# A bidirectional scan on one core: keys and queries of a half head in one tile, and a copy moved to ScalarE

## The chip, the core and the metric

The kernel runs on one core of a Trainium2 chip. A core has five engines, each with a queue of its own that is worked off in order: TensorE (PE in the profile; PEld is its loading of weights), VectorE (DVE), ScalarE (ACT), GpSimd (POOL) and SyncE (SP), which here issues most of the DMAs. Engines meet at semaphores only. The metric is the device time of one execution in microseconds; the time before is a median of three runs. Tiles lie in SBUF, 128 partitions wide; TensorE writes to PSUM, which is handed out here in banks of 128 x 512 float32.

## What is computed

One layer of a hybrid encoder over 1024 positions of width 1024: a norm, one large projection, a convolution module, a bidirectional gated scan over 8 heads of 128, a gated merge, and a feed-forward part. The change lies in the scan. For each head and direction, cut from the reference:

```python
def step(state, inp):                       # one chunk of 64 positions
    qb, kb, vb, lfb = inp
    a = jnp.cumsum(lfb, axis=2)             # lf = log f, f the forget gate
    diff = a[:, :, :, None, :] - a[:, :, None, :, :]
    decay = jnp.where(tril, jnp.exp(jnp.minimum(diff, 0.0)), 0.0)
    scores = jnp.einsum("bhtk,bhsk,bhtsk->bhts", qb, kb, decay)
    o = (jnp.einsum("bhts,bhsv->bhtv", scores, vb)
         + jnp.einsum("bhtk,bhkv->bhtv", qb * jnp.exp(a), state))
    ...
o_fwd = _chunk_gated_scan(qh, heads(k_f), vh, heads(lf_f))
o_bwd = flip(_chunk_gated_scan(flip(qh), flip(heads(k_b)), flip(vh), flip(heads(lf_b))))
return o_fwd + o_bwd
```

So a score of query t and key s carries the product of the forget gates between them, for each of 128 channels; the forward direction takes s up to t, the backward one the rest, and the two sums are added.

## The kernel before

The scan (lines 1053 to 1418) works on half heads: 512 positions of one head, channels on the partitions, both directions at once. There are 16 of them (i = 0 to 15). Four generators work on each.

*scan_inputs* (L1053) loads q and the two gate tiles z (page "zi", three buffers), and ScalarE makes from them the key gates kk (L1064) and the forget gates f (L1065, L1067), which VectorE clamps (L1074). It is called two half heads ahead.

*scan_base* (L1077) works out decays within blocks of 8 positions. All of it is on VectorE. DE holds, for both directions, running products from the middle of each block outwards (E, rows 0 to 3 and on) and the same for D; one buffer for all half heads. The first instruction of a base copies two rows of f into DE (L1092); the second (written as the first tt, L1093) multiplies two rows of f; the third (L1095, in the profile DE<-f,DE) goes on from there, the fourth (L1096) finishes the block products, and the reciprocal (L1098) turns them round. Then come fm, the table tb of block decays, the remaining rows of DE, the scaled queries Qh and keys Kh, and last the queries qF and the keys kG, each a tile of two rows of 512: qF[:, 1] holds the queries of the forward and qF[:, 0] those of the backward direction, kG[:, d] the keys of direction d. qF has three buffers (the outputs of the head read it late), kG two. The helper tt writes every such product at L1042, so the profile names these groups by their tiles.

*scan_levels* (L1137) makes the scores. Within blocks of 8, TensorE multiplies Qh and Kh (inside, L1174). Then for h = 8, 16, 32, 64 it multiplies the keys of each block of h with the queries of its neighbour. At h = 8 and 16 (level, L1157) ScalarE first gathers the keys of a level into a tile A (L1160), and TensorE multiplies A with views of qF (L1162), into a bank "sc" at 8 and "ob" at 16. At 32 and 64 (blocks, L1182) it reads kG and qF directly (L1188). After each level the keys and queries are multiplied by the decay over the neighbouring block, half the blocks of each direction, 512 elements each (L1213 for the keys, L1214 for the queries), and the table is halved (L1222). Masked copies (L1226 to L1230) gather the scores of the lower levels from the banks into D.

*scan_states* (L1238) transposes the updated keys (TensorE L1245, ScalarE's copy kT L1247), multiplies them with the values (L1254, banks "ob" and "sc"), and carries the state: the forward states Sf on VectorE (L1260, L1262), the backward ones Sb copied by ScalarE (L1272, L1274) and carried by VectorE at the start of the outputs (L1347).

*scan_outputs* (L1277) multiplies scores and states (L1295, bank "ob", which has one buffer), takes the norm on ScalarE with GpSimd's power (L1300, L509, L510, L1314), transposes (L1321) and gates the result on VectorE (L1323).

What sets the order: TensorE's order is the program's (manual_schedule). After each step of levels and states, between() puts in 1.3 pieces of the stream "dense" on average (one piece is six 128 x 512 matmuls of the projection's last columns, L147 to L149), two steps of the next half head's base, and one step of the previous head's outputs. The other engines' orders are made when the program is built: a scheduler may move an instruction ahead of others on its engine where its operands allow. The weights of the dense stream are loaded by SP (L134, two buffers), split into a high and a low part by ScalarE and VectorE (L123), and its results are copied out by ScalarE (L720, L722).

The loop around it:

```python
def between(fill):
    dense.fill(fill)
    if ahead is not None:
        ahead.step(BASE_STEPS)
    pending.fill(1)
```

Of the kernel before, what the change touches and what calls it, by code (L numbers as in the profile page):

```python
# [10 lines left out]
F32 = mybir.dt.float32  # L11
# [7 lines left out]
P = 128  # L19
# [11 lines left out]
H = 512  # L31
# [15 lines left out]
def tile_hybrid_encoder(  # L47
# [45 lines left out]
    def nm(s):  # L93
        uid[0] += 1
        return f"{s}_{uid[0]}"
# [6 lines left out]
    def page(pool, tag, bufs, dt=F32):  # L102
        return pool.tile([P, H], dt, tag=tag, name=nm(tag), bufs=bufs)
# [949 lines left out]
    def scan_inputs(i):  # L1053


        h, half = divmod(i, 2)
        q = page(hp, "q", 2)
        f = hp.tile([P, 2, H], F32, tag="f", name=nm("f"), bufs=2)
        kk = hp.tile([P, 2, H], F32, tag="k", name=nm("k"), bufs=2)
        nc.sync.dma_start(q, d_q[h][half])  # L1060
        for d in range(2):
            z = page(hp, "zi", 3)
            nc.sync.dma_start(z, d_z[d][h][half])
# [3 lines left out]
            A.activation(  # L1067
                fo,
                z.rearrange("p (b e) -> p b e", e=8),
                AF.Identity,  # L1070
                scale=oml_of(d, h),
                bias=lb_of(d, h),
            )
        V.tensor_scalar(f, f, MIN_FORGET, 1.0, op0=ALU.max, op1=ALU.min)  # L1074
        return q, f, kk, kscale[:, h : h + NH + 1 : NH]

    def scan_base(ins):  # L1077


        q, f, kk, ks = ins  # L1080

        def two(t, *r):
            if len(r) == 1:
                return view(t, r[0], [[8, N2]])
            return view(t, r[0], [[r[1] - r[0], 2], [8, N2]])

        fv = lambda *r: two(f, *r)
        ed = lambda *r: two(DE, *r)
        D = D0


        V.tensor_copy(ed(2, D + 4), fv(3, 4))  # L1092
# [5 lines left out]
        V.reciprocal(ed(D, 7), ed(0, D + 7))  # L1098
# [36 lines left out]
        yield qF, kG, [(Qh[:, 1 - d, :], Kh[:, d, :]) for d in range(2)], tb  # L1135

    def scan_levels(base, S_t, Tt):  # L1137


        qF, kG, qk, tb = base  # L1140
# [16 lines left out]
        def level(b, h):  # L1157

            A_t = page(hp, "A", 2)
            A.copy(A_t.rearrange("p (b x e) -> p b x e", x=2, e=h), pairs(kG, h))  # L1160
            for at, g, o in each():
                T.matmul(  # L1162
                    b[g, o].rearrange("p (b x e) -> p b x e", x=2, e=h),
                    A_t[:, at : at + 32],
                    view(qF, at, [[2 * h, 16 // h], [H + h, 2], [1, h]]),
                    start=True,
                    stop=True,
                )
# [13 lines left out]
        def blocks(b, h):  # L1182

            for c in range(0, H, P):
                for s0 in range(0, P, h):
                    t0 = s0 ^ h
                    d = s0 // h % 2
                    T.matmul(  # L1188
                        b[s0 : s0 + h, c + t0 : c + t0 + h],
                        kG[:, d, c + s0 : c + s0 + h],  # L1190
                        qF[:, 1 - d, c + t0 : c + t0 + h],
                        start=True,
                        stop=True,
                    )
# [7 lines left out]
        for h in (8, 16, 32, 64):  # L1202
# [5 lines left out]
            else:  # L1208
# [1 line left out]
                    b = bank("sc")  # L1210
                    T.matmul(b, none[:, :P], none, start=True, stop=True)
                blocks(b, h)
            tt(pairs(kG, h), pairs(kG, h), view(tb, 1, [[2, n], [nb - 1, 2], [0, h]]))  # L1213
            tt(pairs(qF, h), pairs(qF, h), view(tb, nb + 1, [[2, n], [nb - 1, 2], [0, h]]))  # L1214
            if h < 64:
                tn = hp.tile([P, 3, NB], F32, tag="tb", name=nm("tb"), bufs=3)
                k = 3
# [17 lines left out]
                    A.copy(S_t[g : g + 32, :, g : g + 32], D_t[g : g + 32])  # L1235
            yield

    def scan_states(i, kG, v, Tt, Sf, Sb):  # L1238

        half = i % 2  # L1240
        kTs = []
        for d in range(2):
            b = bank("tr")
            for c in range(4):
                T.transpose(b[:, c * P : (c + 1) * P], kG[:, d, c * P : (c + 1) * P], ident)  # L1245
            kT = page(hp, "kT", 2)
            A.copy(kT, b)  # L1247
            kTs.append(kT)
            yield
# [27 lines left out]
    def scan_outputs(h, kept, Sf, Sb):  # L1277
# [3 lines left out]
        ss = cp.tile([P, 2, 4], F32, name=nm("oss"), tag="oss", bufs=2)  # L1281
        rs = cp.tile([P, 2, 4], F32, name=nm("ors"), tag="ors", bufs=2)
        for half in range(2):
            S_t, v, qF = kept[half]
            o = bank("ob")
            for c in range(4):
                sl = slice(c * P, (c + 1) * P)
                g = half * 4 + c
                terms = [(S_t[:, c, :], v[:, c, :])]
                if g > 0:  # L1290
                    terms.append((qF[:, 1, sl], Sf[half][:, c, :]))
                if g < 7:
                    terms.append((qF[:, 0, sl], Sb[half][:, c, :]))
                for n, (l, r) in enumerate(terms):
                    T.matmul(o[:, sl], l, r, start=(n == 0), stop=(n == len(terms) - 1))  # L1295
            on = tmp()
# [72 lines left out]
    for h in range(NH):  # L1369
# [4 lines left out]
        for half in range(2):  # L1374
# [13 lines left out]
            for n, _ in enumerate(scan_levels(base, S_t, Tt[:, half])):  # L1388
# [7 lines left out]
            qF, kG = base[0], base[1]  # L1396
            for _ in scan_states(i, kG, v, Tt, Sf, Sb):
                between(FILL)
            kept.append((S_t, v, qF))
            cur = ahead  # L1400
        pending = Stream(outputs(h, kept, Tt, Sf, Sb))

# [397 lines left out]
```

## Time and profile before

| | |
|---|---|
| time before, median of 3 runs (lowest to highest) | 1792.36 us (1791.06 to 1793.42) |
| span of the profiled execution | 1788.8 us |
| instructions | 27583 |
| granted TensorE clock, mean | 0.996 |
| the scan in the span | some 505 to 905 us |
| projections before it, merge and feed-forward after it | the rest |

The profiled execution's own time is not listed beside its span; the runs are 3.6 us above the span. On the page, a group is given by line, engine and operation, output tile <- input tiles, and partitions x elements of each; behind it busy time, mean duration in ns, and the engine's idle time just before with what ended it. In the timeline the columns are start and duration in us, engine, line, operation and tiles; a bracket names idle time before. Instructions of VectorE and ScalarE overlap a little in their records, so the time that one takes in a queue is read from start to start.

### The profile page before, as it was taken

Reading aid. Unit: us, or ns where it says so; the run is one execution under the profiler, and the core shown is the slowest. Engines: PE = TensorE matmul, PEld = TensorE weight load, DVE = VectorE, ACT = ScalarE, POOL = GpSimd, SP = SyncE. Lnnn points to the kernel's source line nnn. Section 1 sums busy time; section 2 is a strip of 40 time slices with the busy share of each in tenths; the row PEclk is TensorE's granted clock in tenths of the full one; section 3 lists DMA queues with packets and bytes.
Section 4 is the critical chain, followed back from the end, with each engine's and each line's share of the span. In section 5 each row is a group of like instructions: output and inputs, shape, how many; then the busy total and the mean of one; then the engine's idle time right before and its main releaser. Section 6 shows DMA issues by size and latency. Waiting matters only on the chain.

```text
span 1788.8 us, 27583 instructions
## 1 busy us (share of the span) xinstructions
PE 1733.0 (97%) x10632; PEld 1416.7 (79%) x10638; DVE 1250.4 (70%) x1884; ACT 775.0 (43%) x1490; POOL 153.8 (9%) x168
## 2 busy tenths in 40 slices
PE   8989999999999999999999999999999999999997
PEld 6878877888777777777778888878888888888885
DVE  5599999746569999999645557667667667544455
ACT  7344333334555566655442245344344344422123
POOL 2201111000000000000000002011111111000000
PEclk9999999999999999999999999999999999999999
DMA  8657887743663433333257665567667665534233
GB/s 285 216 151 187 185 185 185 199 150 126 199 214 101 125 119 119 119 119 101 90 180 219 200 201 177 153 142 159 151 144 158 142 151 133 161 103 126 79 91 135
DMA packets 317705, 276.41 MB, mean 155 GB/s; under 512 B 14462, under 2 KB 242566, under 8 KB 317574
## 3 DMA queue, kind: packets, MB, share of 16 engines
q1 hardware_dynamic: 276406, 242.15, 43.1%
q0 software_dynamic: 41168, 32.51, 12.6%
q8 instruction: 83, 1.36, 0.3%
q14 instruction: 48, 0.39, 0.1%
HBM read 185.73 MB, written 72.61 MB: 144 GB/s over the span
## 4 chain that ended last, share of the span: by engine, by line
PE 65%; DVE 19%; DMA 5%; issue 4%; ACT 4%; POOL 1%; SPq 0%; POOLq 0%; DVEq 0%; ACTq 0%
PE mm L147 16%; PE mm L148 16%; PE mm L149 16%; PE sc L147 3%; PE sc L149 3%; PE sc L148 3%; DVE acc L955 2%; DVE kG L1042 2%; DVE DE L1042 2%; DVE qF L1042 2%; DVE wp L123 2%; PE tr L147 1%; PE tr L149 1%; PE tr L148 1%; DVE DE L1098 1%
## 5 line engine op out<-in xcount | busy, mean ns | idle before, releaser
L147 PE MATMUL mm<-hx,wp 128*128 128x512 f32 x1128 | 454.8, 403 | 9.8 <-DVE ev L717 4.3
L149 PE MATMUL mm<-hx,wp 128*128 128x512 f32 x1128 | 441.7, 392 | 1.9 <-DVE wp L123 1.9
L148 PE MATMUL mm<-hx,wp 128*128 128x512 f32 x1128 | 441.4, 391 | 0.0
L123 ACT CAST wp<-wr 128x1024 fp32r<-128x1024 f32 (+2 forms) x179 | 167.0, 934 | 359.6 <-PE mm L148 271.5
L147 PEld LDWEIGHTS mm<-hx,wp 128*128 128x128 f32 x1128 | 212.5, 188 | 55.7 <-DVE ev L717 6.7
L123 DVE TENSOR_TENSOR wp<-wr,wp 128x1024 fp32r<-128x1024 f32 (+2 forms) x177 | 191.4, 1082 | 90.4 <-ACT wp L123 90.1
L149 PEld LDWEIGHTS mm<-hx,wp 128*128 128x128 f32 x1128 | 212.6, 188 | 49.3 <-DVE wp L123 3.2
L148 PEld LDWEIGHTS mm<-hx,wp 128*128 128x128 f32 x1128 | 212.9, 189 | 40.4 <-issue 0.2
L955 DVE SCALAR_TENSOR_TENSOR acc<-gl,v_b,acc 128x1024 f32<-128x1024 f32 x120 | 149.0, 1277 | 0.5
L1651 DVE TENSOR_TENSOR xr<-mm,xr 128x512 f32<-128x512 f32 x48 | 33.2, 691 | 73.1 <-PE mm L149 73.1
L367 ACT COPY su<-mm 128x512 f32<-128x512 f32 x78 | 45.2, 579 | 62.5 <-PE mm L149 61.5
L123 ACT CAST wq<-sw 128x1024 fp32r<-128x1024 f32 x39 | 41.0, 1051 | 64.4 <-issue 28.6
L1500 DVE SCALAR_TENSOR_TENSOR tm<-gp,v_a,tm 128x512 f32<-128x512 f32 x88 | 65.9, 749 | 2.0
L147 PE MATMUL mm<-hy,wp 128*128 128x512 f32 x156 | 61.5, 394 | 1.4 <-ACT su L367 1.4
L148 PE MATMUL mm<-hy,wp 128*128 128x512 f32 x156 | 61.1, 392 | 0.0
L147 PE MATMUL sc<-hy,wq 128*128 128x512 f32 x156 | 61.1, 392 | 0.0
L149 PE MATMUL sc<-hy,wq 128*128 128x512 f32 x156 | 61.1, 391 | 0.0
L147 PE MATMUL tr<-hx,wp 128*128 128x512 f32 x156 | 60.8, 390 | 0.0
L149 PE MATMUL tr<-hx,wp 128*128 128x512 f32 x156 | 60.7, 389 | 0.0
L148 PE MATMUL tr<-hx,wp 128*128 128x512 f32 x156 | 60.7, 389 | 0.0
L148 PE MATMUL sc<-hy,wq 128*128 128x512 f32 x156 | 60.7, 389 | 0.0
L149 PE MATMUL mm<-hy,wp 128*128 128x512 f32 x156 | 60.6, 389 | 0.0
(368 smaller groups left out, 3467.6 us busy)
## 6 DMA issues: line engine op xcount, KB each, us to landing
wr<-in_w_in_dram SPq DMA_DIRECT2D x56, 512.0 KB, 4.7
wr<-in_ffn_w_up_dram SPq DMA_DIRECT2D x24, 512.0 KB, 4.9
sw<-in_ffn_w_up_dram SPq DMA_DIRECT2D x44, 256.0 KB, 3.0
d_g<-ft SPq DMA_DIRECT2D x44, 256.0 KB, 2.7
sw<-in_ffn_w_up_dram POOLq DMA_DIRECT2D x20, 512.0 KB, 8.3
sw<-in_w_in_dram SPq DMA_DIRECT2D x34, 256.0 KB, 3.2
d_z<-ev SPq DMA_DIRECT2D x32, 256.0 KB, 3.1
zi<-d_z SPq DMA_DIRECT2D x32, 256.0 KB, 3.2
```

The source lines that it names most:

```text
L123: parts = A.copy(hi, src), eng.tensor_tensor(lo, src, hi.bitcast(F32), op=ALU.subtract)
L147: T.matmul(acc, whi[:, k, :], ahi, start=first, stop=False, skip_group_check=again)
L148: T.matmul(acc, whi[:, k, :], alo, start=False, stop=False, skip_group_check=again)
L149: T.matmul(acc, wlo[:, k, :], ahi, start=False, stop=last, skip_group_check=again)
L367: A.copy(t, acc)
L955: V.scalar_tensor_tensor(acc, g[:, k : k + S], tap(k), acc, op0=ALU.mult, op1=ALU.add)
L1042: V.tensor_tensor(o, a, b, op=op)
L1098: V.reciprocal(ed(D, 7), ed(0, D + 7))
L1500: V.scalar_tensor_tensor(c, g[:, o + k : o + k + H], vec("fdw", k * NF + j), c, op0=ALU.mult, op1=ALU.add,)
L1651: V.tensor_tensor(xr[i][half], acc, xr[i][half], op=ALU.add)
```

## The change

Keys and queries of a half head lie in one tile KQ of four rows, keys and queries by turns: row 0 the keys of the forward direction, row 1 the queries of the backward one, row 2 the keys of the backward, row 3 the queries of the forward direction. With that, the blocks that a level's update touches in the keys and in the queries form one regular view: pairs(h, n) runs over n steps of 2h, across two neighbouring rows, in rows 0 and 1 and, shifted by h, in rows 2 and 3. One instruction of 1024 elements takes the place of two of 512 after each level. KQ has three buffers (24 KB of each partition, where qF and kG took 20), and zi two in place of three. The copy at the start of a base goes from VectorE to ScalarE. What is computed stays the same.

```diff
@@ scan_inputs
-            z = page(hp, "zi", 3)
+            z = page(hp, "zi", 2)
@@ scan_base
-        V.tensor_copy(ed(2, D + 4), fv(3, 4))
+        A.copy(ed(2, D + 4), fv(3, 4))
         tt(ed(1, D + 5), fv(2, 4), fv(3, 5))
         yield
         tt(ed(0, D + 6), fv(1, 6), ed(1, D + 5))
...
-        qF = hp.tile([P, 2, H], F32, tag="qF", name=nm("qF"), bufs=3)
-        kG = hp.tile([P, 2, H], F32, tag="kG", name=nm("kG"), bufs=2)
+        KQ = hp.tile([P, 4, H], F32, tag="KQ", name=nm("KQ"), bufs=3)
...
-        both = [[H, 2], [8, NB], [1, 8]]
-        tt(view(qF, 0, both), view(Qh, 0, both), view(fm, 0, [[NB, 2], [1, NB], [0, 8]]))
+        both, apart = [[H, 2], [8, NB], [1, 8]], [[2 * H, 2], [8, NB], [1, 8]]
+        tt(view(KQ, H, apart), view(Qh, 0, both), view(fm, 0, [[NB, 2], [1, NB], [0, 8]]))
         yield
-        tt(view(kG, 0, both), view(Kh, 0, both), view(DE, D + 7, [[H, 2], [8, NB], [0, 8]]))
+        tt(view(KQ, 0, apart), view(Kh, 0, both), view(DE, D + 7, [[H, 2], [8, NB], [0, 8]]))
@@ scan_levels
-        def pairs(t, h):
-            return view(t, 0, [[2 * h, H // (2 * h)], [H + h, 2], [1, h]])
+        def pairs(h, n):
+            return view(KQ, 0, [[2 * h, n], [2 * H + h, 2], [1, h]])
...
-            A.copy(A_t.rearrange("p (b x e) -> p b x e", x=2, e=h), pairs(kG, h))
+            A.copy(A_t.rearrange("p (b x e) -> p b x e", x=2, e=h), pairs(h, H // (2 * h)))
...
-                    view(qF, at, [[2 * h, 16 // h], [H + h, 2], [1, h]]),
+                    view(KQ, H + at, [[2 * h, 16 // h], [2 * H + h, 2], [1, h]]),
...
-            tt(pairs(kG, h), pairs(kG, h), view(tb, 1, [[2, n], [nb - 1, 2], [0, h]]))
-            tt(pairs(qF, h), pairs(qF, h), view(tb, nb + 1, [[2, n], [nb - 1, 2], [0, h]]))
+            tt(pairs(h, nb), pairs(h, nb), view(tb, 1, [[2, nb], [nb - 1, 2], [0, h]]))
```

In blocks, scan_states and scan_outputs the views follow: kG[:, d] is KQ[:, 2 * d], qF[:, 1 - d] is KQ[:, 3 - 2 * d].

More of the change, by code (lines that the diff above doesn't have):

```diff
@@ L1129, in scan_base @@
             yield
-        both = [[H, 2], [8, NB], [1, 8]]
-        tt(view(qF, 0, both), view(Qh, 0, both), view(fm, 0, [[NB, 2], [1, NB], [0, 8]]))
+        both, apart = [[H, 2], [8, NB], [1, 8]], [[2 * H, 2], [8, NB], [1, 8]]
+        tt(view(KQ, H, apart), view(Qh, 0, both), view(fm, 0, [[NB, 2], [1, NB], [0, 8]]))
         yield
-        tt(view(kG, 0, both), view(Kh, 0, both), view(DE, D + 7, [[H, 2], [8, NB], [0, 8]]))
+        tt(view(KQ, 0, apart), view(Kh, 0, both), view(DE, D + 7, [[H, 2], [8, NB], [0, 8]]))
         yield
-        yield qF, kG, [(Qh[:, 1 - d, :], Kh[:, d, :]) for d in range(2)], tb
+        yield KQ, [(Qh[:, 1 - d, :], Kh[:, d, :]) for d in range(2)], tb
     def scan_levels(base, S_t, Tt):
-        qF, kG, qk, tb = base
-        def pairs(t, h):
-            return view(t, 0, [[2 * h, H // (2 * h)], [H + h, 2], [1, h]])
+        KQ, qk, tb = base
+        def pairs(h, n):
+            return view(KQ, 0, [[2 * h, n], [2 * H + h, 2], [1, h]])
         def near(t):
@@ L1236, in scan_levels, with scan_states @@
             yield
-    def scan_states(i, kG, v, Tt, Sf, Sb):
+    def scan_states(i, KQ, v, Tt, Sf, Sb):
         half = i % 2
@@ L1244, in scan_states @@
             for c in range(4):
-                T.transpose(b[:, c * P : (c + 1) * P], kG[:, d, c * P : (c + 1) * P], ident)
+                T.transpose(b[:, c * P : (c + 1) * P], KQ[:, 2 * d, c * P : (c + 1) * P], ident)
             kT = page(hp, "kT", 2)
@@ L1283, in scan_outputs @@
         for half in range(2):
-            S_t, v, qF = kept[half]
+            S_t, v, KQ = kept[half]
             o = bank("ob")
@@ L1290, in scan_outputs @@
                 if g > 0:
-                    terms.append((qF[:, 1, sl], Sf[half][:, c, :]))
+                    terms.append((KQ[:, 3, sl], Sf[half][:, c, :]))
                 if g < 7:
-                    terms.append((qF[:, 0, sl], Sb[half][:, c, :]))
+                    terms.append((KQ[:, 1, sl], Sb[half][:, c, :]))
                 for n, (l, r) in enumerate(terms):
@@ L1395, in tile_hybrid_encoder @@
                 between(FILL)
-            qF, kG = base[0], base[1]
-            for _ in scan_states(i, kG, v, Tt, Sf, Sb):
+            KQ = base[0]
+            for _ in scan_states(i, KQ, v, Tt, Sf, Sb):
                 between(FILL)
-            kept.append((S_t, v, qF))
+            kept.append((S_t, v, KQ))
             cur = ahead
```

4 lines of the change are left out of this document (2 added, 2 removed).

## The prediction

> **What bounds the kernel now.** I read the page first (first lines, then the strip of VectorE over the span), then the scan by stretches of 120 us, then who waited there.
>
> ```profile
> span 1788.8 us, 27583 instructions
> PE 1733.0 (97%) x10632; PEld 1416.7 (79%) x10638; DVE 1250.4 (70%) x1884; ACT 775.0 (43%) x1490; POOL 153.8 (9%) x168
> ...
> DVE  5599999746569999999645557667667667544455
> ```
>
> The whole span belongs to TensorE (97%). Only in two places is VectorE full; the second, slices 12 to 19, is the scan. The same stretch by windows (columns: stretch, length, then busy microseconds and instructions of each engine, clock, DMA):
>
> ```profile
> 520.00:640.00 120.00, 113.04 (x1419) 92.02 (x1421) 112.40 (x223) 70.73 (x166) 3.98 (x4) 1.00 0.38 115
> 640.00:760.00 120.00, 113.59 (x1527) 93.05 (x1527) 111.56 (x227) 71.27 (x172) 4.18 (x4) 1.00 0.40 124
> 760.00:880.00 120.00, 114.88 (x1486) 94.30 (x1487) 104.35 (x219) 65.48 (x174) 5.57 (x6) 1.00 0.31 100
> ```
>
> Two engines are nearly full at once: TensorE for 341.5 of 360 us, VectorE for 328.3; ScalarE is at 58%. The change leaves TensorE's instructions and their order as they are, so the time can move only through TensorE's idle time, 18.5 us here. What ended it, over the same 360 us (engine and line, what it waited for, us in total, times, longest):
>
> ```profile
> PE ob L1162 <- DVE qF L1042: 6.0, 7, 1.5
> PE tr L1245 <- DVE kG L1042: 4.9, 7, 1.8
> PE sc L1188 <- DVE qF L1042: 3.2, 6, 1.2
> PE ob L1295 <- DVE D L1230: 1.1, 1, 1.1
> PE sc L1254 <- ACT kT L1247: 0.9, 2, 0.5
> PE ob L1162 <- ACT wp L123: 0.9, 1, 0.9
> ```
>
> Nearly all of it is VectorE being late, in three places of a half head: before the matmuls of level 16 (6.9), before the key transposes (4.9), before levels 32 and 64 (3.2). Each is a wait between two engines, so it depends on where VectorE's work stands in its queue as well as on how much there is.
>
> **The change part by part.**
>
> ```profile
> L1042 DVE TENSOR_TENSOR qF<-qF,tb 128x512 f32<-128x512 f32 x62 | 42.4, 684 | 0.4 <-PE sc L1162 0.4
> L1042 DVE TENSOR_TENSOR kG<-kG,tb 128x512 f32<-128x512 f32 x62 | 42.2, 682 | 0.6 <-ACT A L1160 0.4
> ...
> L1160 ACT COPY A<-kG 128x512 f32<-128x512 f32 x32 | 19.7, 616 | 20.9 <-DVE kG L1042 20.8
> L1042 DVE TENSOR_TENSOR qF<-Qh,fm 128x1024 f32<-128x1024 f32 x16 | 19.5, 1218 | 0.0
> ...
> L1092 DVE COPY DE<-f 128x256 f32<-128x256 f32 x15 | 6.3, 418 | 0.0
> ...
> L1225 ACT COPY D<-sc 128x128 f32<-128x128 f32 x16 | 4.2, 265 | 5.8 <-PE sc L1162 5.7
> ```
>
> (The groups of the scan, mean ns behind the busy time.) *Work off VectorE.* 64 pairs of 512-element updates become 64 of 1024. By durations that is 683+683-1218 = 148 ns each. But a row runs on into the next one; what the queue gets back is start to start, from the timeline of the fifth half head:
>
> ```profile
> 610.25 1.21 DVE L1042 TENSOR_TENSOR kG<-Kh,DE 128x1024 f32<-128x1024 f32 x1
> 611.38 0.41 DVE L1092 COPY DE<-f 128x256 f32<-128x256 f32 x1
> 611.71 0.71 DVE L1042 TENSOR_TENSOR DE<-f 128x256 f32<-128x256 f32 x1
> ...
> 612.45 0.69 DVE L1042 TENSOR_TENSOR DE<-f,DE 128x256 f32<-128x256 f32 x1
> 613.18 0.40 DVE L1042 TENSOR_TENSOR DE<-DE,f 128x128 f32<-128x128 f32 x1
> 613.61 1.76 DVE L1098 RECIPROCAL DE<-DE 128x256 f32<-128x256 f32 x1
> 615.28 0.25 DVE L1262 SCALAR_TENSOR_TENSOR Sf<-Sf,Tt,ob 128x128 f32<-128x128 f32 x1
> ...
> 616.05 0.34 DVE L1262 SCALAR_TENSOR_TENSOR Sf<-Sf,Tt,ob 128x128 f32<-128x128 f32 x1
> 616.30 1.22 DVE L123 TENSOR_TENSOR wp<-wr,wp 128x1024 fp32r<-128x1024 f32 x1
> 617.44 0.34 DVE L1262 SCALAR_TENSOR_TENSOR Sf<-Sf,Tt,ob 128x128 f32<-128x128 f32 x1
> 617.70 0.69 DVE L1042 TENSOR_TENSOR kG<-kG,tb 128x512 f32<-128x512 f32 x1
> 618.30 0.34 DVE L1347 SCALAR_TENSOR_TENSOR Sb<-Sb,Tt 128x128 f32<-128x128 f32 x1
> ...
> 618.90 0.69 DVE L1042 TENSOR_TENSOR qF<-qF,tb 128x512 f32<-128x512 f32 x1
> ```
>
> 1024 elements take 1.13 us (610.25 to 611.38), 512 take 0.60 (617.70 to 618.30): 0.07 us a pair, 4.5 us for 64. The copy gives 0.33 (611.38 to 611.71), 5.3 for 16. Together 9.8 us, 0.6 for a half head. On ScalarE the copy costs between the 265 ns of 128 elements and the 616 of 512, taken at 0.38, so 6 us on an engine at 58%; its own load is no bound.
>
> *What the order makes of it.* In the program before, the keys' update of level 8 or 16 waits only for ScalarE's copy A; after, it rewrites the queries too and must wait for TensorE's level. And level 16 now runs through VectorE (level 8's merged update), ScalarE (copy A of level 16) and then TensorE. The bigger shift is the copy's: the third instruction of a base (the 612.45 row) waits, in the built program, for ScalarE's copy, which stands there behind copy A of the half head just begun. So in 12 of 15 half heads the built order puts that instruction, the next and the reciprocal behind the forward state update, where they stood ahead of it. That update waits for TensorE's state matmuls:
>
> ```profile
> 613.06 1.05 PE L1254 MATMUL ob<-v,kT 128*128 128x128 f32 x8
> ...
> 616.91 0.45 PE L1162 MATMUL sc<-qF,A 128*32 128x32 f32 x30
> ...
> 618.56 0.40 PE L149 MATMUL mm<-hx,wp 128*128 128x512 f32 x1
> 619.74 0.46 PE L1162 MATMUL ob<-qF,A 128*32 128x32 f32 x32 [0.78 <-DVE qF L1042]
> ```
>
> Before, the states end at 614.11, VectorE comes 1.17 us late to them (615.28) because it is finishing the reciprocal, and ends the queries' update at 619.59; TensorE, free at 618.96, waits 0.78. After: without copy, third and fourth instruction and reciprocal VectorE is there before 613.1 and idles. From 614.15 it does, start to start: three state updates (0.77), the weight split (1.14), third (0.73) and fourth (0.43) instruction, two backward updates (0.52), reciprocal (1.67), the merged update (1.21): 6.5 us, to 620.6. Copy A takes 0.62 and the handovers some 0.2: TensorE starts at 621.4, a wait of 2.4 for 0.78, so 1.6 more. Done so for each half head from the two built orders, the mean shift is 1.4 us. Six of the twelve have no slack there (they wait today): 8.4. In two, four transposes of the outputs stand in the gap, whose 0.53 us come off the shift, 0.9 each: 1.8.
>
> ```profile
> 645.02 0.60 PE L1321 MATMUL tr<-ident,tm 128*128 128x128 f32 x4
> 645.55 0.46 PE L1162 MATMUL ob<-qF,A 128*32 128x32 f32 x32
> ```
>
> Four have dense matmuls enough to hide it. Two that wait today and keep their order give back what the copy and a pair free, 0.4 each. **Term 1: +9.4.** Low end -3 (VectorE remains late at the states, the reorder costs nothing and the shorter queue gives half a microsecond in six), high end +20 (twelve pay 1.7 in full).
>
> *The bank "ob".* The output matmuls of the previous head wait until the masked copy has read level 16 (the row of 1.1). That copy now stands behind a merged update that can only start when level 16 is done: some 0.5 us late in seven half heads, less the 1.1 of today. **Term 2: +2.4**, from -1.1 to +5.
>
> *Waits that go.* A TensorE that is held at level 16 gives VectorE the time to be ready later: some 1.2 us (0.6 of work, and its update of level 8 ends earlier by copy A's 0.62 before TensorE's start). Against it the transposes wait for 1.13 us of update where they waited for the keys' 0.60. Of 4.9+3.2 us I take 6.5 away. **Term 3: -6.5**, from -8.1 to 0.
>
> The Trainium skill, page "Perfetto Trace Analysis", section "Optimizing Scalar/DVE Operations", has a rule for either side: larger operations help an engine that is saturated, while one that is not but leaves bubbles on others had better be given smaller ones, so that parts are done sooner. By the second half the update should have stayed in two: with 16 transposes each 0.53 later Term 3 would be +8.5, and the time 1812.7, which I count to the much slower cases below.
>
> *At nothing:* two buffers of zi for three, and KQ in three buffers.
>
> ```profile
> SPq L1063 <- ACT f L1067: 60.1, 25, 5.7
> ...
> ACT wp L123 <- PE mm L148: 11.1, 6, 3.8
> ```
>
> Between 480 and 900 us SP's queue already waits 60 us for a free zi, and the weight loads stand behind it; but ScalarE's split of weights waits for TensorE to free a page, not for a load. In the built order the weight load now comes ahead of most zi loads. Were that cover gone, a load would be late by up to the 5.7 us of the longest wait. KQ is held as long as qF was, in as many buffers.
>
> Sum: +9.4+2.4-6.5 = +5.3 on the span of 1788.8, which the median of the runs shown, 1792.36, exceeds by 3.6: **1797.7 us**.
>
> **The rivals.** *Faster: VectorE is the bound and 9.8 us come off.* For it: 94% and 93% busy in the first two stretches, and nearly every TensorE wait is for it. Against: TensorE has only 18.5 us to give and is 95% busy itself, and the reciprocal stands later. It decides if VectorE still reaches the state update late: then 1782.5. By its first half, the rule of the Trainium skill named above would have it so.
>
> *Much slower: the copy is late in ScalarE's queue.* In three half heads it stands behind the scaling of the outputs, which waits for GpSimd. Today the clamp pays for that place:
>
> ```profile
> DVE f L1074 <- ACT f L1067: 9.8, 4, 4.0
> ```
>
> 2.45 us each; three such and some 0.3 in twelve others add 11 to the forecast: 1808.7.
>
> *No change: waits only trade places.* If the shift is 0.7 rather than 1.4, Term 1 is 4.2 and the sum 0.1: 1792.4. For it speaks that VectorE's lateness is a matter of a microsecond either way; against it, that the reciprocal alone is longer than the shift.
>
> *It doesn't do what it says:* the merged update, over four rows in place, could take as long as two old rows, 1.36 us. It would then cost 0.16 more than a pair instead of 0.07 less, 14.7 us more in VectorE's queue than I have counted; a quarter of it shown gives 1801.4, within the forecast's range.
>
> **How the numbers follow.** The forecast, 1796 to 1803, has 0.40; much slower (above that) 0.15; no change, within 3.6 us or 0.2%, about what a measurement of this kernel tells from none, 0.22; faster 0.23. So faster 0.23, same 0.22, slower 0.55. The range takes in most of the rivals on both sides, 1784 to 1809; the forecast's own is given above.
>
> **What would show it.** Right: in the profile after, the reciprocal behind the first state update; VectorE idle before that update, waiting for TensorE's states; TensorE's wait at level 16, now for copy A of ScalarE, near 16 us in place of 6.9; its waits for transposes and at levels 32 and 64 near 2; TensorE busy as before, VectorE about 16 us less by durations. Wrong: level 16's wait at or under 7 (Term 1), transposes that wait 5 or more (Term 3), long waits of the third base instruction for ScalarE's copy (the second rival), or a merged update over 1.3 us.

## The result, and the profile after

| | before | after |
|---|---|---|
| median of 4 runs each (lowest to highest), us | 1792.89 (1791.06 to 1794.90) | 1822.85 (1821.26 to 1827.04) |
| span of the profiled execution, us | 1788.8 | 1825.3 |
| mean granted TensorE clock | 0.996 | 0.988 |

The ratio after to before is 1.0164, 95% interval 1.0143 to 1.0185: slower, by 30 us where +5 was forecast. The profiled execution after is the longest of the four (1827.04), so the spans differ by 36.5 us where the medians differ by 30. The page's first lines and VectorE's strip over the span:

```profile
span 1825.3 us, 27537 instructions
PE 1749.4 (96%) x10638; PEld 1424.6 (78%) x10638; DVE 1240.1 (68%) x1804; ACT 786.0 (43%) x1506; POOL 152.9 (8%) x168
...
DVE  5599998656479778878735656866666766545455
```

VectorE has less work by 10.3 us and 80 instructions, as meant. TensorE has the same matmuls (six of their records are missing before) and is busy 16.4 us longer. The scan by stretches of 120 us, columns as before:

```profile
520.00:640.00 120.00, 105.52 (x1299) 84.01 (x1299) 103.36 (x192) 61.60 (x133) 1.84 (x2) 0.96 0.34 104
640.00:760.00 120.00, 110.69 (x1397) 91.13 (x1397) 95.46 (x173) 74.41 (x190) 5.50 (x6) 0.99 0.35 112
760.00:880.00 120.00, 109.07 (x1300) 88.61 (x1298) 102.81 (x187) 66.86 (x160) 3.67 (x4) 0.96 0.34 108
```

Neither engine is full now, so it isn't a shortage of either: they wait for each other. And the clock, 1.00 throughout the scan before, is 0.96 in two stretches. The windows of both kernels over the same work, from the first matmul of the first half head's level 8 to the start of the last one's level 16, before first:

```profile
529.80:878.99 349.19, 330.70 (x4311) 270.56 (x4305) 317.68 (x653) 201.45 (x500) 13.72 (x14) 1.00 0.35 111
```

```profile
531.56:911.38 379.82, 343.40 (x4317) 279.01 (x4304) 312.34 (x578) 211.98 (x516) 12.85 (x14) 0.96 0.33 104
```

30.6 of the 36.5 us are here: TensorE's idle time went from 18.5 to 36.4 (length less busy time), +17.9, and its busy time grew by 12.7 for the same matmuls. What ended the idle time in the scan after:

```profile
PE ob L1161 <- ACT A L1159: 30.5, 15, 3.6
PE tr L1243 <- DVE KQ L1042: 2.7, 5, 0.9
PE ob L1293 <- DVE D L1228: 2.3, 3, 1.4
PE sc L1252 <- ACT kT L1245: 0.8, 3, 0.3
```

Nearly all of the growth is at one place, level 16, from 6.8 us in all to 30.5; the bank "ob" adds 1.2, the other waits shrink (line numbers are one or two lower than before). The fifth half head, which the prediction worked through, in the timeline (rows of VectorE, ScalarE and TensorE):

```profile
625.72 0.69 DVE L1074 TENSOR_SCALAR f<-f 128x1024 f32<-128x1024 f32 x1 [2.30 <-ACT f L1067]
626.33 0.72 DVE L1260 SCALAR_TENSOR_TENSOR Sf<-Sf,Tt,ob 128x128 f32<-128x128 f32 x2
627.16 1.23 DVE L123 TENSOR_TENSOR wp<-wr,wp 128x1024 fp32r<-128x1024 f32 x1
...
628.56 0.67 DVE L1042 TENSOR_TENSOR DE<-f,DE 128x256 f32<-128x256 f32 x1
...
629.40 0.45 DVE L1042 TENSOR_TENSOR DE<-DE,f 128x128 f32<-128x128 f32 x1
...
630.02 1.74 DVE L1098 RECIPROCAL DE<-DE 128x256 f32<-128x256 f32 x1
...
630.38 0.40 PE L149 MATMUL mm<-hx,wp 128*128 128x512 f32 x1
631.69 1.15 DVE L1042 TENSOR_TENSOR KQ<-KQ,tb 128x1024 f32<-128x1024 f32 x1
...
632.87 0.62 ACT L1159 COPY A<-KQ 128x512 f32<-128x512 f32 x1 [3.39 <-DVE KQ L1042]
...
633.54 0.65 PE L1161 MATMUL ob<-KQ,A 128*32 128x32 f32 x32 [2.77 <-ACT A L1159]
```

Read from the bottom: level 16 waited 2.77 us (0.78 before) for copy A, which waited for the merged update, which stood behind the reciprocal, which stood behind the state updates and the weight split. That is the chain of the prediction, link by link; it gave 2.4 us. One thing differs at its head: VectorE did not idle there for TensorE's states but for the clamp's input from ScalarE (2.30 us, the first row), and the state update started behind the clamp, 0.40 us after the states' end at 625.93.

The clock, in the sixth half head: columns as above, the clock is the third figure from the end.

```profile
659.80:663.20 3.40, 0.00 (x0) 0.00 (x0) 3.40 (x5) 0.62 (x1) 0.00 (x0) 1.00 0.38 110
663.20:664.20 1.00, 0.95 (x34) 0.83 (x35) 0.96 (x4) 0.00 (x0) 0.00 (x0) 1.00 0.65 231
664.20:667.60 3.40, 3.40 (x9) 2.61 (x8) 3.37 (x11) 0.60 (x1) 0.00 (x0) 0.50 0.43 156
667.60:671.00 3.40, 3.40 (x52) 2.31 (x52) 3.03 (x5) 0.59 (x1) 0.00 (x0) 0.99 0.21 81
```

TensorE idles at level 16, and within a microsecond of its restart the clock is at one half for 3.4 us: 9 dense matmuls in that time. In windows of half a microsecond there are eight such falls in the scan after, up to the last level 16, and none before. At half the clock, 3.4 us hold 1.7 us less of work, eight falls 13.6: that fits the 12.7 by which the busy time grew.

### The profile page after: what moved, and what is told of

Same layout as the page of the kernel before. It is cut to its first block, busy times and chain, and to the rows that moved or that the text cites. A ratio compares the mean times of both kernels' runs of the same rounds, so it can differ in the third digit from the quotient of the medians.

```text
span 1825.3 us, 27537 instructions
## 1 busy us (share of the span) xinstructions
PE 1749.4 (96%) x10638; PEld 1424.6 (78%) x10638; DVE 1240.1 (68%) x1804; ACT 786.0 (43%) x1506; POOL 152.9 (8%) x168
## 4 chain that ended last, share of the span: by engine, by line
PE 57%; DVE 16%; DMA 12%; ACT 8%; issue 5%; POOL 1%; SPq 0%; POOLq 0%; DVEq 0%; ACTq 0%
PE mm L147 15%; PE mm L149 14%; PE mm L148 14%; DMA wr<-wr 3%; DVE acc L955 3%; DMA sw<-in_ffn_w_up_dram 2%; DMA wr<-sw 2%; PE sc L147 2%; DVE KQ L1042 2%; PE sc L149 2%; PE sc L148 2%; DVE wp L123 2%; DVE DE L1042 1%; DMA sw<-in_w_in_dram 1%; PE ob L1293 1%
## 5 line engine op out<-in xcount | busy, mean ns | idle before, releaser
L147 PE MATMUL mm<-hx,wp 128*128 128x512 f32 x1128 | 459.4, 407 | 12.6 <-DVE ev L717 6.4
L147 PEld LDWEIGHTS mm<-hx,wp 128*128 128x128 f32 x1128 | 214.7, 190 | 60.6 <-DVE ev L717 9.0
L149 PEld LDWEIGHTS mm<-hx,wp 128*128 128x128 f32 x1128 | 214.6, 190 | 51.8 <-DVE wp L123 4.9
L148 PEld LDWEIGHTS mm<-hx,wp 128*128 128x128 f32 x1128 | 215.3, 191 | 40.8 <-issue 0.2
L1042 DVE TENSOR_TENSOR KQ<-KQ,tb 128x1024 f32<-128x1024 f32 x64 | 77.9, 1217 | 8.3 <-PE sc L1187 7.8
L147 PE MATMUL mm<-hy,wp 128*128 128x512 f32 x156 | 61.6, 395 | 1.4 <-ACT su L367 1.4
L148 PE MATMUL mm<-hy,wp 128*128 128x512 f32 x156 | 61.2, 392 | 0.0
```

The source lines that it names most:

```text
L147: T.matmul(acc, whi[:, k, :], ahi, start=first, stop=False, skip_group_check=again)
L148: T.matmul(acc, whi[:, k, :], alo, start=False, stop=False, skip_group_check=again)
L149: T.matmul(acc, wlo[:, k, :], ahi, start=False, stop=last, skip_group_check=again)
L1042: V.tensor_tensor(o, a, b, op=op)
```

## The experiments

Thirteen kernels, each beside runs of the kernel before on the same chip. "Stall" is the sum of the 16 waits at level 16 in the profiled scan, "falls" are those of the clock before the last level 16; both are of one execution each. e9 to e12 and e14 follow further down.

| kernel | copy on | updates | median us | ratio, 95% interval | stall us | falls |
|---|---|---|---|---|---|---|
| before | VectorE | two | 1792.9 | 1 | 6.8 | 0 |
| after | ScalarE | merged | 1822.9 | 1.0164 (1.0143 to 1.0185) | 30.5 | 8 |
| e3 | VectorE | two | 1790.0 | 0.9977 (0.9967 to 0.9987) | 9.7 | 1 |
| e1 | VectorE | merged | 1802.3 | 1.0047 (1.0025 to 1.0069) | 12.6 | 2 |
| e7 | ScalarE | two | 1815.4 | 1.0119 (1.0093 to 1.0146) | 27.2 | 4 |
| e2 | ScalarE | two, two tiles | 1807.1 | 1.0073 (1.0058 to 1.0088) | 12.5 | 0 |
| e8 | ScalarE, split | merged | 1794.6 | 0.9996 (0.9987 to 1.0005) | 11.4 | 0 |
| e13 | VectorE, base split | merged | 1794.8 | 1.0003 (0.9994 to 1.0012) | 11.9 | 1 |
| e8b | ScalarE, split | merged at 32, 64 | 1788.1 | 0.9962 (0.9947 to 0.9977) | 6.7 | 0 |
| e5 | VectorE | merged at 32, 64 | 1793.4 | 0.9989 (0.9979 to 1.0000) | 7.8 | 0 |

**Which part of the change.** e1, e3 and e7 with the kernel after make a square on the common tile: the copy on either engine, the updates merged or not.

```diff
# e1: the changed kernel with
-        A.copy(ed(2, D + 4), fv(3, 4))
+        V.tensor_copy(ed(2, D + 4), fv(3, 4))
# e7: the changed kernel with (e3: both edits)
-            tt(pairs(h, nb), pairs(h, nb), view(tb, 1, [[2, nb], [nb - 1, 2], [0, h]]))
+            for o, r in ((0, 1), (H, nb + 1)):
+                x = view(KQ, o, [[2 * h, n], [2 * H + h, 2], [1, h]])
+                tt(x, x, view(tb, r, [[2, n], [nb - 1, 2], [0, h]]))
# e2: the kernel before with
-        V.tensor_copy(ed(2, D + 4), fv(3, 4))
+        A.copy(ed(2, D + 4), fv(3, 4))
```

> The changed kernel with only the copy of the first decays given back to VectorE; the interleaved tile, the merged updates and two buffers of zi stay. In the built order the reciprocal then stands ahead of the forward state update in nearly all half heads. Theory 1 (the copy's handover put the reciprocal behind the states, and that makes the level-16 wait): that wait falls from 30 us to 10 or less, and the time to 1786 to 1794 us. Theory 2 (the merged update itself: level 8's update, copy A and level 16 in one chain): the level-16 wait stays above 20 us and the time above 1812. Theory 3 (the granted TensorE clock falls where TensorE stalls over 2 us): whichever it is, the clock in the scan is 1.00 if no level-16 wait exceeds 1.5 us and below 0.98 if several exceed 2.5 us.

> Only the interleaved tile and two buffers of zi: the keys' and the queries' updates stay two instructions for a level (on the common tile), the copy is VectorE's. Theories 1 and 2 both: 1790 to 1796 us, level-16 wait near 7 us. If instead the tile itself is the cause (other rows read by TensorE, waits counted by tile rather than by part): a level-16 wait above 15 us or TensorE's matmuls of the scan more than 2 per cent longer, and 1805 us or more.

> The changed kernel with its merged updates taken apart again into two instructions on the common tile; the copy stays on ScalarE. Theory 1 (the copy): 1812 to 1830 us, level-16 wait above 20 us, granted clock in the scan 0.98 or lower. Theory 2 (the merged update): 1790 to 1797 us, level-16 wait near 7 us, clock 1.00. With each cause holding half: 1800 to 1810.

> The kernel before with only the copy of the first decays moved to ScalarE; keys and queries keep their tiles and separate updates, zi its three buffers. The built order moves third and fourth base instruction and reciprocal further back here, among or behind the updates of the next half head's levels 8 and 16. Theory 1 (the copy is the cause): slower than before, 1800 to 1825 us, with waits at levels 16 or 32 and transposes that sum to 20 us more. Theory 2 (merged update is the cause): 1786 to 1793 us, waits as before. Theory 3: the clock in the scan below 0.99 only if single stalls exceed 2 us.

By ratios, the copy's move costs 0.0142 with two updates (e3 to e7) and 0.0117 with merged ones (e1 to after), 25 and 21 us. Merging costs 0.0070 with the copy on VectorE (e3 to e1) and 0.0045 with it on ScalarE, 13 and 8 us (the last with intervals that just meet). Both causes are real, the copy's is about twice the other, and together they give the whole. Theory 1 has the larger half; its range for e1 was missed by 8 us, because merging isn't free. The tile and the two zi buffers alone cost nothing (e3 is 0.0023 or 4 us under before; level-16 wait 9.7, 2.7 above what was expected). The level-16 and transpose waits of e7, e1 and e3 (TensorE's waits in the scan, columns as before):

```profile
PE ob L1161 <- ACT A L1159: 27.2, 14, 3.4
...
PE tr L1245 <- DVE KQ L1042: 0.2, 1, 0.2
```

```profile
PE ob L1161 <- ACT A L1159: 12.6, 10, 1.9
PE tr L1243 <- DVE KQ L1042: 8.4, 7, 2.2
```

```profile
PE ob L1161 <- ACT A L1159: 9.7, 8, 1.9
...
PE tr L1245 <- DVE KQ L1042: 2.0, 4, 0.6
```

The two causes show at different places. The copy makes the stall at level 16 (9.7 to 27.2). Merging makes the key transposes wait (2.0 to 8.4), in two ways: they wait for the queries' half of the last update as well, and in four half heads (3, 5, 7 and 13, with 7.6 of the 8.4 us) e1's built order puts that update behind the whole reciprocal, where e3's two stand ahead of it. In e5 below the merged update stands ahead of the reciprocal too, and the transposes wait 5.0. Where TensorE is already held at level 16 they wait little (0.2 in e7, 2.7 in the kernel after).

In e2 the copy has no merged update beside it, and its wait takes another form: the built order there puts third instruction and reciprocal among the next half head's updates, and TensorE also waits at levels 8, 32 and 64.

```profile
PE ob L1162 <- DVE qF L1042: 12.5, 10, 2.7
PE sc L1188 <- DVE qF L1042: 6.4, 9, 1.4
PE sc L1162 <- ACT A L1160: 4.4, 4, 2.1
```

Its time fell in the range of theory 1; all of TensorE's waits together grew by some 11 us, not by the 20 expected.

**The copy's wait, or its load.** The copy writes row 2 of E and row 4 of D, for both directions. The third instruction reads E's row 1 and D's row 5 and writes E's row 0 and D's row 6: it needs nothing of the copy. The built program makes it wait all the same; with views of one row each it doesn't. (The halves of the split are E's and D's, not the two directions, as the first expectation below has it.)

```diff
# e8: the changed kernel with (e13: with the second and third edit, and the copy whole on VectorE)
-        A.copy(ed(2, D + 4), fv(3, 4))
+        A.copy(ed(2), fv(3))
+        A.copy(ed(D + 4), fv(4))
-        tt(ed(0, D + 6), fv(1, 6), ed(1, D + 5))
+        tt(ed(0), fv(1), ed(1))
+        tt(ed(D + 6), fv(6), ed(D + 5))
-        V.reciprocal(ed(D, 7), ed(0, D + 7))
+        V.reciprocal(ed(D), ed(0))
+        V.reciprocal(ed(7), ed(D + 7))
```

> The changed kernel, copy still on ScalarE and updates merged, but the copy, the third base instruction and the reciprocal are each split into their two halves (one of the forward, one of the backward decays). The third base instruction reads nothing that the copy writes; with views of one stride the built program no longer makes it wait for ScalarE, and the reciprocal stands ahead of the state update again. ScalarE's load is as before the split or higher (two copies of 128 elements, 265 ns each, for one of 256); VectorE gets about 0.3 us more for a half head from the split and loses the 0.33 of the copy. Theory 1a (the wait of the third instruction and the reordering it causes are what the copy costs): 1797 to 1806 us, level-16 wait 9 to 15 us, as with the copy on VectorE. Theory 1b (ScalarE's load or its place in ScalarE's queue is the cost): above 1814 us and a level-16 wait above 20.

> The control for the split: merged updates at all levels, the copy whole and on VectorE, but third base instruction and reciprocal split into halves as in the split kernel. Unsplit, with the copy on VectorE, the time was 1802.3; split, with the copy on ScalarE, 1794.6. If the split itself only costs VectorE its 0.3 us for a half head: 1801 to 1807 us, level-16 wait 12 to 16, and the copy's move is worth some 8 us once nothing waits for it. If the split helps by itself (halves of the reciprocal let the state update and the merged update in between): 1793 to 1798, level-16 wait 9 to 12, and the copy's move is worth nothing that can be measured.

e8 takes back the whole loss: 1794.6, below what either theory gave. ScalarE's load is no smaller (its two half copies take 458 and 461 ns, the whole one 711), so theory 1b has fallen. But e13, the control, is as fast with the copy on VectorE: so the split helps by itself, by 0.0044 or 8 us (e1 to e13), and the copy's engine makes no difference that can be measured once nothing waits for it. Of the 30 us between after and e8, then, some 21 are the wait and 8 the split. That is by subtraction: no run with the copy on ScalarE takes the wait away without the split, and none tells VectorE's waiting itself (9.0 us in the scan after, shown below) from the order that was built around it. Waits of e8, then of e13:

```profile
PE ob L1164 <- ACT A L1162: 11.2, 9, 1.9
PE tr L1246 <- DVE KQ L1042: 3.5, 7, 0.7
```

```profile
PE ob L1163 <- ACT A L1161: 11.7, 10, 1.9
PE tr L1245 <- DVE KQ L1042: 4.4, 7, 1.2
```

Against e1 it is the transposes that wait less (8.4 to 4.4): in the four half heads named above the merged update of level 64 stood behind the whole reciprocal, 1.76 us; in e13 it stands behind one of its halves only, 0.95 each, and the four waits come to 3.5 us in place of 7.6. The clock falls once less before the last level 16 and once less behind it. That the order makes the difference is read from the orders, not tried alone.

**Where merging costs.** e5 and e8b merge at levels 32 and 64 only, e8b on e8, e5 on e1. After level 8, ScalarE's copy A for level 16 needs only the keys' half of the update; and after 8 and 16 the keys' half can start behind copy A, where the merged update waits for TensorE's level too.

> As the split kernel (copy on ScalarE without the wait), with merged updates only at levels 32 and 64 and two updates at levels 8 and 16. If waits at level 16 come only from the wait and from the merged update of level 8: 1785 to 1791 us, level-16 wait 6 to 10 us, clock 1.00. If merging at 32 and 64 or the copy on ScalarE costs by itself: 1795 or more.

> Interleaved tile, copy on VectorE, merged updates only at levels 32 and 64, two at 8 and 16. Theory (merging costs where TensorE waits for the keys' half alone, at levels 8 and 16 and not after): 1786 to 1791 us, level-16 wait 8 to 11 us, as with the tile alone. Rival (merging costs at the last levels as well, since the key transposes wait for the keys' half alone at level 64): transposes wait 6 us or more, and 1793 to 1800 us.

e8b is 0.0034 or 6 us under e8: merging at levels 8 and 16 costs that, and the level-16 wait falls with it (11.4 to 6.7). Its ratio excludes 1, so it beats both kernels.

```profile
PE ob L1164 <- ACT A L1162: 6.6, 7, 1.4
PE tr L1251 <- DVE KQ L1042: 3.5, 5, 1.0
```

e5 came out 2 us above the theory's range, at the low end of the rival's, with transposes at 5.0 us where the rival had 6 or more. Merging late may cost a little too: 0.0012 or 2 us against e3, with intervals that overlap. e12 is the other half of e8b, the kernel before with only e8's split and copy on ScalarE; e11 is e8b with the dense work dealt out otherwise:

```diff
# e11: e8b with
-                between(FILL)
+                between(2.0 if n == 0 else FILL - 0.1)
...
-                between(FILL)
+                between(FILL - 0.1)
```

> The kernel before with only the copy of the first decays on ScalarE, with copy, third base instruction and reciprocal split into halves so that VectorE needn't wait for it; keys and queries in two tiles, two updates for each level. If the gain of the split kernels comes from the copy that VectorE no longer makes: 1786 to 1792 us here too, against 1807 for the copy on ScalarE unsplit. If the interleaved tile and the merged updates of levels 32 and 64 are needed for it: 1793 to 1798.

> As the split kernel with merged updates only at levels 32 and 64 (1788.1 us), but the dense work that TensorE gets between the stages of a half head is dealt out differently: always two blocks of six matmuls (1.28 us each) between levels 8 and 16 in place of one or two, and so much less behind the other stages; the total is as before. If the remaining level-16 waits (6.6 us, 7 times) are VectorE's lateness at that place alone, they fall to 1 us or less, and the time to 1781 to 1786. If VectorE is simply short of time, the waits move to the key transposes and levels 32 and 64: 1787 to 1792.

e12 took 1790.0 us, 0.9977 (0.9963 to 0.9991), in the first theory's range: neither the common tile nor the merged updates are needed. That the gain is the copy's is not shown: e13 found none from the copy's move, and the split of the kernel before with the copy on VectorE was not run. e11 took 1791.6, 0.9986 (0.9975 to 0.9997), in the rival's range: level 16 no longer waits (0.02 us), but the waits moved to the transposes and to the outputs' bank, not to levels 32 and 64 (0.6 us), and up to the last level 16 TensorE idles as long as in e8b (13.5 and 13.8 us). What e11 takes longer than e8b came behind that: the transposes of the last outputs wait 4.8 us (2.1 in e8b), and the clock is at one half there for 6.8 us.

```profile
PE tr L1251 <- DVE KQ L1042: 6.9, 8, 1.6
PE tr L1327 <- ACT tm L1320: 4.8, 1, 4.8
PE ob L1301 <- DVE D L1236: 3.5, 5, 1.2
```

**The clock.** Three kernels fill the stalls of the changed kernel with matmuls of zeros: three of them ahead of every level 16 (e9), eight in the 12 half heads with long stalls (e10), six in the eight with a fall (e14). The edit of e9:

```diff
                     b = bank("ob")
+                    for _ in range(3):
+                        T.matmul(b, none[:, :P], none, start=True, stop=True)
```

> The changed kernel with three matmuls of zeros (128x512, 0.39 us each in the profile before) ahead of level 16's matmuls, into its bank, which level 16 then overwrites. VectorE's and ScalarE's work and waits stay. They fill 1.2 us of each level-16 stall. Theory 3 (TensorE's idle time in the stalls makes the granted clock fall, eight times to one half for 3.4 us in the scan of the changed kernel, 1.7 us each): the falls vanish all or nearly, the scan runs at 0.99 or 1.00, and the time falls by 9 to 14 us to 1809 to 1815, though TensorE got 19 us more work, nearly all of it in idle time. Rival (the clock falls for another reason, or the fall costs nothing that counts): time 1820 us or more, clock in the scan still 0.96 to 0.97.

> The changed kernel with eight matmuls of zeros ahead of level 16 (three took 0.65 us of TensorE's time in the run with three, so eight 1.7 us), only in the 12 half heads whose level-16 stall was over 1.6 us in the changed kernel. Theory 3 (idle time in a stall makes the granted clock fall, some 1.7 us each): no fall or at most one in the scan, its mean clock 0.99 or 1.00, and the time 10 to 14 us under the changed kernel's 1822.8, so 1809 to 1813. Rival (falls are not from the idle time, or what a fall costs is waited for anyway): falls stay, or they go and the time stays at 1818 or more.

> The changed kernel with six matmuls of zeros (0.215 us each, 1.3 us) ahead of level 16 only in the eight half heads behind whose stall the granted clock fell; unlike in the run with eight zero matmuls, the built order of ScalarE is unchanged and VectorE's nearly so (16 of 1776 instructions moved). Theory 3 (the falls' 12.7 us are a cost of their own): at most two falls in the scan, and a ratio to the kernel before of 1.007 to 1.010 (1805 to 1812 us) in place of 1.0164. Rival (where the clock falls, TensorE would have waited for VectorE soon after anyway, at levels 16 or 32): falls go, and the ratio stays at 1.013 or more, with the missing time in TensorE's waits for the merged updates and for level 16.

| | median us | ratio, 95% interval | falls in the scan |
|---|---|---|---|
| after | 1822.9 | 1.0164 (1.0143 to 1.0185) | 8 |
| e9 | 1820.7 | 1.0143 (1.0127 to 1.0160) | 3 |
| e10 | 1821.1 | 1.0156 (1.0130 to 1.0183) | 1 |
| e14 | 1816.4 | 1.0119 (1.0102 to 1.0137) | 3 |

Most falls go when the idle time is filled, so they come from it. What they cost is less plain. The intervals of e9 and e10 overlap that of after. e9 has five falls fewer in its profiled execution, as e14 has, but came out only 0.0021 or 4 us faster: it filled 0.65 us where 1.2 was meant, and in four half heads there was no stall over 0.6 us to fill. In e10, whose VectorE order had moved, the gain turned into waits elsewhere:

```profile
PE ob L1298 <- DVE D L1233: 5.9, 5, 1.5
PE sc L1189 <- DVE KQ L1042: 5.7, 5, 2.0
PE ob L1163 <- ACT A L1161: 5.0, 7, 1.8
```

e14 keeps the orders but for 16 instructions of VectorE, and is 0.0045 or 8 us faster than after, with intervals that don't meet: five falls fewer, 1.6 us each if the gain is all theirs. Its scan over the same work:

```profile
531.77:905.99 374.22, 345.22 (x4352) 277.52 (x4353) 312.57 (x577) 211.82 (x516) 12.84 (x14) 0.99 0.33 105
```

Less the 11.1 us that the records of the zeros cover, TensorE's busy time is 334.1: 9.3 under after. The stretch is 5.6 shorter, so in this one execution 3.7 went into longer waiting. Theory 3's range was missed by 4 us, with three falls left. So e14 speaks for a cost of the falls' own, some 8 us for five of them. How much of the 12.7 is lost time in the kernel after stays open: e9 and e10, with as few falls or fewer, gained nothing that can be told from none.

## Why the prediction was wrong

*Term 1 failed in its size, not in its mechanism.* It gave +9.4 us for the wait at level 16, up to +20; it grew from 6.8 to 30.5, +23.7. The chain is as described, and in the twelve half heads (2 to 13) the reciprocal stands behind the first state update as said. By the parts of the step:

| half heads | forecast, us | measured, us |
|---|---|---|
| 3, 4, 5, 7, 11, 13 (waited before, reordered) | +8.4 | +10.0 |
| 2, 6, 8, 9, 10, 12 (waited nothing, reordered) | +1.8 | +10.3 |
| 1 and 15 (waited before, order kept) | -0.8 | +3.1 |
| 14 and 16 | 0 | +0.4 |

The largest error is the second row: these half heads were taken as covered, wholly ("four have dense matmuls enough to hide it") or in part, and 2, 6, 10 and 12 wait 1.7, 3.5, 2.3 and 2.1 after. In 2, 6 and 12 VectorE had been ready only 0.1 to 0.4 us before TensorE. A stall of zero in the row isn't slack; the end of the update beside the start of the matmuls would have told. And "the mean shift is 1.4 us" was too small: from the end of the state matmuls to the moment when level 16's operands are ready, the twelve shifted by 2.2 us on average, those six by 2.7.

*What the sum of work left out is VectorE's waiting for ScalarE.* The step had VectorE ready before the states end ("is there before 613.1 and idles"). In eight of the twelve half heads it was; in 4, 5, 6 and 12 its first state update starts 1.95, 0.40, 1.60 and 2.16 us after them, because it was held by the third instruction (7.3 us), the clamp (2.3), the weight split (6.5) and the clamp (7.6). And once the reciprocal is behind the state update, every wait in between delays it. VectorE's waits for ScalarE in the scan after:

```profile
DVE f L1074 <- ACT f L1067: 17.4, 10, 7.6
DVE wp L123 <- ACT wp L123: 15.3, 4, 6.5
...
DVE DE L1042 <- ACT DE L1092: 9.0, 8, 7.3
```

The clamp waited 9.8 us before and the weight split 7.7. Between the first state update and the merged update of the twelve, clamp and third instruction wait 5.4 us (2.0 before), 2.12 of it for the clamp of the tenth half head. The late starts and this growth together, 9.5 us, are about what the twelve shifted beyond the 16.8 of the forecast (26.6). Why 1 and 15 wait longer was not traced.

*The price of the copy* was taken at 0.38 us, between rows of 128 and 512 elements that lie side by side, or in runs. The copy's elements lie eight apart, and it takes 0.71:

```profile
L1092 ACT COPY DE<-f 128x256 f32<-128x256 f32 x16 | 11.4, 711 | 0.0
```

On VectorE the same strided view took 0.42. By e8, where two halves take 0.92 together, this hardly counts.

*The clock was not in the sum at all.* "TensorE busy as before" was wrong by 12.7 us in the scan. With 17.9 of idle time it makes the 30.6 of the scan; by e14 at least part of it is time of its own.

*Term 2 and Term 3* stayed in their ranges: bank "ob" from 1.1 to 2.3 (+1.2 for +2.4); transposes and levels 32 and 64 from 8.1 to 2.7 (-5.4 for -6.5). But Term 3 is no gain of the merged update. e1 shows that without the stall ahead of them the transposes wait 8.4 us. There the second half of the rule in the Trainium skill ("Perfetto Trace Analysis", section "Optimizing Scalar/DVE Operations"), that on an engine which isn't full but leaves bubbles on others instructions are better broken up, agrees with the runs: merging cost 13 us for 64 instructions saved (e3 to e1). Its first half, that larger ones help a saturated engine, gave nothing here, though VectorE was up to 94% busy.

*VectorE's own saving* was as said: a merged update takes 1217 ns, as the 1218 of the row it was priced by.

```profile
L1042 DVE TENSOR_TENSOR KQ<-KQ,tb 128x1024 f32<-128x1024 f32 x64 | 77.9, 1217 | 8.3 <-PE sc L1187 7.8
```

*The rivals.* Faster, no change and a slow merged update are out. The much slower one, the copy late behind the output scaling, happened once instead of three times, in the fourth half head, where the third instruction waited 7.3 us:

```profile
600.06 1.28 ACT L1312 ACTIVATE tm<-tm,ors 128x128 f32<-128x128 f32 x4
601.24 0.69 ACT L1092 COPY DE<-f 128x256 f32<-128x256 f32 x1
```

It had the right part of the change. That its price for three such places, 7.35 us, is near the one wait is luck: level 16 of that half head waited only 1.9 us more than before. Its sum fell short because it carried the same Term 1, and no case had the clock.

*Open:* the 5.9 us of the span outside the compared stretch (1.8 ahead of it, 4.1 behind). Behind it the clock falls once more, at 940.7 us of the span after and not before, at most 1.7 us; the rest was not traced.

## What to carry to other kernels

When an instruction moves to another engine, price the new edge, not the work: here a wait that the data didn't need, and the order of VectorE's queue that was built around it, cost some 21 us, and both were gone with views of one row each. Ask of each wait in the new program whether its operands need it. And merge two instructions only where no one waits for the first of them alone; after level 8 the keys' half alone was what ScalarE's copy needed next, and after level 64 what the transposes needed.

## What the hardware showed that was not expected

The clock falls after stalls of 1.7 us and more, but other stalls left no fall: 2.5 us in the seventh half head, 2.1 in the twelfth, 3.4 in the first of e7. In the scan falls last 3.41 us at one half (twice that in e11), and start at multiples of 3.41 us apart (609.6, 633.5, 664.2, 763.2, 787.1: 7, 9, 29 and 7 times). Cut into windows of that length, with the falls' starts as bounds, the traces show what counts. The fifteenth half head with the shortest stall (1.69 us, to 885.08) and its fall, and the twelfth (2.12 us, to 814.79) without one:

```profile
882.68:886.09 3.41, 1.73 (x39) 1.12 (x38) 3.38 (x10) 0.62 (x1) 0.00 (x0) 1.00 0.11 37
886.09:889.50 3.41, 3.41 (x10) 2.67 (x9) 3.41 (x9) 0.00 (x0) 0.00 (x0) 0.50 0.02 5
```

```profile
811.00:814.41 3.41, 1.68 (x10) 1.18 (x8) 3.41 (x6) 0.29 (x1) 0.00 (x0) 1.00 0.11 28
814.41:817.83 3.42, 3.04 (x76) 2.29 (x76) 3.42 (x10) 0.33 (x1) 0.00 (x0) 1.00 0.99 336
```

TensorE is busy for 0.51 and 0.49 of the windows ahead: at about half, either happens. Over the fifteen traces, from 515 to 945 us of each span, there are 34 falls, each behind a window that was busy for 0.18 to 0.51; behind a window of 0.42 or less the clock was always at one half, behind one of 0.52 or more never. The 3.4 us of e7 lay across two windows, busy for 0.53 and 0.49. So the idle share of a fixed window decides, not the length of the stall. The Trainium skill, page "TensorE: Matmul & The Clock Gate", has such a free-running window and the half rate (section "What's actually happening"); the traces agree. Its rule that idle gaps over about 3.4 us are what bites (section "HAM oscillation — how this bites in real kernels") is too mild here: a window half idle was enough, with stalls of half that length.

A copy with a stride of eight elements on ScalarE takes 711 ns for 256 and 458 for 128, 2.0 ns for each further element. Rows without that stride, the 616 for 512 elements in runs and the 265 for 128 read from PSUM, come to 0.9.
